# A hybrid SSM and attention block on one core: the GLU from two steps earlier, squares in tiles of their own, and some adds on another engine

## The chip, the core and the metric

The kernel runs on one core of a Trainium2 chip. The metric is device time in microseconds (us) for one execution. Three runs of the kernel before gave 1503.86, 1506.82 and 1508.20 us; the median is 1506.82. A fourth execution was profiled.

The engines are named as the profile names them: PE is TensorE's matmul and PEld its weight load, DVE is VectorE, ACT is ScalarE, POOL is GpSimd, SP is SyncE, which here only issues transfers. Each engine takes its instructions in the order in which the program holds them; an instruction that waits holds up those behind it on its engine. PSUM is the memory that matmuls write, held here as banks of 128 x 512 fp32; SBUF is the memory of tiles.

## What is computed

One layer over a sequence of 2048 tokens with 1024 channels, cut to what matters:

```python
hn = rmsnorm(h, mix_norm_g)
u, g_ssm, q, k, v, g_attn = split(hn @ w_in)              # six times 512 columns
y = s5_scan(u)                                            # diagonal complex state space model, 32 groups
val, gate = split(gelu(y + d * u) @ w_glu + b_glu)        # 512 -> 2 x 512
y_ssm = val * sigmoid(gate) * silu(g_ssm)
y_att = stick_breaking(rmsnorm(q), rmsnorm(k), v) * silu(g_attn)   # 8 heads of 64, causal
h = h + concat(y_ssm, y_att) @ w_out
h = h + sigmoid(rmsnorm(h, ple_norm_g) @ w_ple_gate) * (p @ w_ple_proj)
```

Stick-breaking attention needs, for each block of 128 queries, the scores, a running sum over the keys from the right (a scan on DVE) and a product with v.

## The kernel before

All matmuls of fp32 data are made of three: each operand is split into a high part (ACT, L513, or L491 where weights are scaled too) and a low part (DVE, L65 or L76) in a matmul format, and high x high, low x high and high x low are summed in PSUM (L541 to L543, and L707 to L709 for the last stages).

**Stages, in the time of the profiled execution.**
- 0 to about 148 us: `phase_u`. The row blocks T (256 tokens each) are loaded, and u = x @ w_in is computed by L541 to L543. The first row block is multiplied before its norm is known: `norms(i)` for its two halves (L573 to L586) computes the squares on ACT (L575), sums them by three adds on POOL (L577) and a matmul with ones (`ps_row`, L579), and spreads the row scale by a second matmul (L585) and an ACT copy (L586). The result scales u afterwards (DVE, `uq`). Later row blocks are normed first (`load_x`, L588 to L603): an ACT square with a sum (L596), a power on POOL (L507), an ACT scaling (L598), transposes on PE (`ps_x`, L526), and the split. Beside all this a long chain of small DVE operations prepares the constants of the scan (`ssm_chain`).
- to about 313 us: the state space model in batches and its output z, and the gate.
- about 313 to 1110 us: the attention loop, steps t = 0 to 39. Four pairs of heads follow each other, each 8 steps after the last, with 16 query blocks each; so two pairs overlap until t = 31, and only the last is left from t = 32. A block's scores go to PSUM (`ps_z`, L812), ACT takes the exponentials (L816), the DVE scans (`px`, L821), PE turns the weights (`ps_wt`, L526), ACT copies them (`ws`, L835), and PE multiplies them with v (`ps_o`, L843). The projections of later blocks (`ps_q`, L745) are laid between.
- In the last eight of these steps (`glu_at = steps - 8`) stands the GLU: 16 units, two each step. Every fourth one starts with `glu_z`, four loads of z (`zt`, two buffers) and their split to `zr` (ACT 513, DVE L65). A unit (`glu_unit`, L684 to L699) has 12 matmuls for the gate half (`ps_g`, bank "ssm") and 12 for the value half (`ps_v`, bank "acc"), a sigmoid on ACT (L696), a DVE multiply-add (L76), a product with the SSM gate on POOL (L698) and a store (L699). The GLU's weights (`wst<-in_ssm_w_glu_dram`) are loaded from step 29 on.
- In the same steps `cross_sums` (L861) makes, in eight groups, sums of blocks of w_out and w_ple_gate by four POOL subtractions each: the last two matrix products are done by a scheme with seven block products instead of eight, which needs such sums of the weights and of the activations.
- about 1110 to 1285 us: the product with w_out for pairs of query blocks (`mixed_pair`, matmuls `ps_h`). Its sums of activations, `sx`, are four POOL adds a pair (L912), split by ACT and DVE to `yr`; then `h<-h,u` on POOL (L969).
- to 1504 us: the gated layer (`gated_pair`, `ps_g`). Its last operations are a DVE product with the projection of p and a POOL add of h (L1026), then the store.

**What sets the order.** The code does not run in the order in which it is written. A planner (`plan`, `list_schedule`, `best_order`, `arrange`) lays out the instructions of each engine from a model of durations and the dependences between instructions, tile reuse among them. So each edit lets it lay out the neighbourhood anew. Tiles come from pools with a fixed count of buffers by tag; a tile that takes a buffer waits until everything that used the one before in it is done. The pool "w" is a ring of 16 weight tiles. The pool kv2 holds, for keys and values, the slots 2, 5, 6 and 7 of the attention; slots 2, 5 and 7 are last read by the third pair of heads, whose last block is at t = 31; slot 6 by the second pair, at t = 23. `BANKS` says which PSUM banks the scores, the projections and the outputs use; the GLU's steps use a set that leaves "ssm" to it.

Of the kernel before, what the change touches and what calls it, by code (L numbers as in the profile page):

```python
# [18 lines left out]
P = 128  # L19
# [7 lines left out]
L = 16  # L27
# [518 lines left out]
def phase_u(e, pool, xp, chain):  # L546
# [23 lines left out]
    ones = pool.tile([P, P], F32, tag="ones", name="ones")  # L570
    nc.gpsimd.memset(ones, 1.0)

    def norms(i):  # L573
        x, r = plain[i], e.rs[i]
        nc.scalar.activation(x, x, AF.Square)  # L575
        for n in (4, 2, 1):
            nc.gpsimd.tensor_tensor(x[:, :n], x[:, :n], x[:, n:2 * n], op=ALU.add)  # L577
        ps = e.bank("ps_row", "tr", "ssm")
        nc.tensor.matmul(ps[:, :1], x[:, 0], ones[:, :1], start=True, stop=True)  # L579
        vs(nc, r, ps[:, :1], 1.0 / DM, ALU.mult, EPS, ALU.add)  # L580
        nc.gpsimd.tensor_tensor(r, r, e.mhalf[:, :1], op=ALU.pow)
        d = pool.tile([P, P], F32, tag="dg", name="dg", bufs=1)
        vs(nc, d, e.ident, r, ALU.mult)
        ps = e.bank("ps_row", "tr", "ssm")
        nc.tensor.matmul(ps[:, :P], ones, d, start=True, stop=True)  # L585
        nc.scalar.activation(e.row[i // 2][:, i % 2 * P:i % 2 * P + P], ps[:, :P], AF.Copy)  # L586
# [84 lines left out]
def glu_z(e, pool, tb):  # L671

    zf = e.z_d.rearrange("j (k p) c -> p k j c", p=P)
    zr = pool.tile([P, 2, 4, 512], F32R, tag="zr", name="zr", bufs=1)
    for k in range(4):
        n = NCH // 4
        zt = pool.tile([P, L, n], F32, tag="zt", name="zt", bufs=2)
        e.nc.sync.dma_start(zt, zf[:, k, :, tb * n:(tb + 1) * n])
        hi, lo = (zr[:, s, k].rearrange("p (c j) -> p c j", j=L) for s in range(2))
        split(e, hi, lo, zt.rearrange("p j c -> p c j"))  # L680
    return zr


def glu_unit(e, pool, w, zr, tb, m):  # L684
    nc = e.nc
    gt = pool.tile([P, 512], F32, tag="gsm", name="gsm", bufs=2)
    nc.sync.dma_start(gt, e.gs_d[tb][m * P:(m + 1) * P])
    pg = e.bank("ps_g2", "ssm")
    pv = e.bank("ps_v2", "acc")
    cs = slice(m * P, (m + 1) * P)  # L690
    for half, ps in ((1, pg), (0, pv)):
        for c in range(4):
            wt = w[half][c]
            mm3(e, ps, (wt[:, 0, cs], wt[:, 1, cs]), (zr[:, 0, c], zr[:, 1, c]), c == 0, c == 3)
    sg = pool.tile([P, 512], F32, tag="glus", name="glus", bufs=2)
    nc.scalar.activation(sg, pg, AF.Sigmoid, bias=e.bglu[:, 4 + m:5 + m])  # L696
    stt(nc, sg, pv, e.bglu[:, m:m + 1], sg, ALU.add, ALU.mult)
    nc.gpsimd.tensor_tensor(sg, sg, gt, op=ALU.mult)  # L698
    nc.sync.dma_start(e.ys_d[tb][m * P:(m + 1) * P], sg)  # L699
# [158 lines left out]
    A.w += load_w(e, [cols[c, :, :, P * A.hp:P * (A.hp + 1)] for c in range(lo, hi)], 512, e.gmix, at=lo, **kw)  # L858


def cross_sums(e, pool, src, dst, scale, c):  # L861

    nc = e.nc
    t = []
    for i, j in ((0, 0), (0, 1), (1, 1), (1, 0)):
        a = pool.tile([P, 512], F32, tag="cs", name="cs", bufs=4)
        k = 4 * i + c
        nc.sync.dma_start(a, src[k * P:(k + 1) * P, 512 * j:512 * j + 512])
        if scale is not None:
            nc.scalar.activation(a, a, AF.Copy, scale=scale[:, k:k + 1])  # L870
        t.append(a)
    b11, b12, b22, b21 = t
    gp = nc.gpsimd.tensor_tensor
    gp(b11, b12, b11, op=ALU.subtract)
    gp(b12, b22, b12, op=ALU.subtract)
    gp(b22, b22, b11, op=ALU.subtract)
    gp(b21, b21, b22, op=ALU.subtract)
    for k, a in enumerate((b11, b22, b12, b21)):
        nc.sync.dma_start(dst[k][c * P:(c + 1) * P], a)
# [20 lines left out]
    return load_w(e, [d[c * P:(c + 1) * P] for c in range(4)], 512, None, **kw)  # L900


def cross_products(e, pool, name, q, w, early, late):

    nc = e.nc

    def f(tag, n):
        return pool.tile([P, 512], F32, tag=tag, name=tag, bufs=n)

    def add(a, b, op=ALU.add):  # L910
        t = f("sx", 3)
        nc.gpsimd.tensor_tensor(t, a, b, op=op)  # L912
        return t

    def product(ps, a, k, first):
        y = pool.tile([P, 2, 4, P], F32R, tag="yr", name="yr", bufs=4)
        split(e, y[:, 0].rearrange("p c t -> p (c t)"), y[:, 1].rearrange("p c t -> p (c t)"), a)
        for c in range(4):
            mm3x(e, ps, (y[:, 0, c], y[:, 1, c]), (w[k][c][:, 0], w[k][c][:, 1]), first and c == 0, c == 3, not first)

    ps = [e.bank(name, "z0", "z1", "acc", "ssm", "w0", "w1") for _ in range(4)]
    product(ps[0], q[0], 0, True)
    s1 = add(q[2], q[3])
    s2 = add(s1, q[0], ALU.subtract)
    r = f("r", 1)
    nc.scalar.activation(r, ps[0], AF.Copy)
    product(ps[1], s2, 1, True)
    u = f("u", 2)
    vt(nc, u, ps[1], r, ALU.add)
    product(ps[2], s1, 2, True)  # L930
    early(u, ps[2], 0)
    s3 = add(q[0], q[2], ALU.subtract)
    product(ps[3], s3, 3, True)
    early(u, ps[3], 1)
    product(ps[0], q[1], 4, False)
    late(0, ps[0], None)
    late(3, None, None)
    s4 = add(q[1], s2, ALU.subtract)
    product(ps[2], s4, 5, False)
    late(1, ps[2], u)  # L940
    product(ps[3], q[3], 6, False)
    late(2, ps[3], u)


def mixed_pair(e, pool, far, j):
# [31 lines left out]
        nc.scalar.activation(jk, h[k], AF.Square, accum_out=ss[:, i, m:m + 1])  # L977
        nc.sync.dma_start(e.h_d[2 * j + i][:, 512 * m:512 * m + 512], h[k])

    cross_products(e, pool, "ps_h", q, e.wo, early, late)  # L980
    r = pool.tile([P, 2], F32, tag=f"rs{j}", name="rs")
    vt(nc, r, ss[:, :, 0], ss[:, :, 1], ALU.add)
    vs(nc, r, r, 1.0 / DM, ALU.mult, EPS, ALU.add)
# [4 lines left out]
def gated_pair(e, pool, far, j, rs):  # L988
# [25 lines left out]
    def late(k, ps, u):  # L1014
# [8 lines left out]
        for c in range(2):  # L1023
            mm3x(e, pp, (pr[:, 0, c, ts], pr[:, 1, c, ts]), (e.wp[m][c][:, 0], e.wp[m][c][:, 1]), c == 0, c == 1)
        vt(nc, o[k], pp, o[k], ALU.mult)
        nc.gpsimd.tensor_tensor(o[k], o[k], h[k], op=ALU.add)  # L1026
        nc.sync.dma_start(e.out[0, (2 * j + i) * P:(2 * j + i + 1) * P, 512 * m:512 * m + 512], o[k])

    cross_products(e, pool, "ps_g", q, e.wg, early, late)
# [15 lines left out]
def hybrid_block_kernel(ctx: ExitStack, tc: tile.TileContext, x, xt, small, p, w_in, ssm_w_glu, w_out, w_ple_gate,  # L1045
# [121 lines left out]
    pk = pool(right, "pack", side="right")  # L1167
    early.close()
    e.stage = e.stage[:1]
    mid = ExitStack()  # L1170
    bp = pool(mid, "pb")
    with e.later():
        wgate = load_w(e, row_blocks(e.w_in[0], NC8, 512), 512, e.gmix)
# [39 lines left out]
    kv1 = pool(far, "kv1", side="right")  # L1213
    ap = pool(far, "attn", side="right")
    steps = NT + SKEW * (NHP - 1)
    glu_at = steps - 8
    for t in range(steps):
        e.z_banks, e.q_banks, e.o_banks = BANKS[2 if t < SKEW - 2 else t >= glu_at]
        for hp in range(NHP):
            if 0 <= t - SKEW * hp < NT:  # L1220
                attn_block(e, ap, A[hp], t - SKEW * hp)
        if t == glu_at:
            left.close()
            gl = pool(left, "glu")
            sums = pool(left, "sums")
        for hp in range(NHP):
            i = t - SKEW * hp
            if 0 <= i + 2 < NT and i + 2 >= (AHEAD if hp == 0 else 0):
# [5 lines left out]
        if t == AHEAD - 1:  # L1234
            left.close()
            e.xp = pool(ctx, "xp")
            kv2 = pool(left, "kv2")
            wx = pool(left, "wx")
        if t == glu_at - 3:
            wglu = glu_load(e)  # L1240
        if t >= glu_at:
            u = 2 * (t - glu_at)
            if u % 4 == 0:
                zr = glu_z(e, gl, u // 4)
            for k in range(u, u + 2):
                glu_unit(e, gl, wglu, zr, k // 4, k % 4)
            c = t - glu_at
            cross_sums(e, sums, *((w_out[0], e.so_d, None) if c < 4 else (w_ple_gate[0], e.sg_d, e.gple)), c % 4)
        if t == steps - 3:
            e.wo = [cross_weights(e, e.w_out[0], e.so_d, None, p) for p in range(2)]  # L1250
            wo4 = cross_weights(e, e.w_out[0], e.so_d, None, 4, pool=Halves(e))
    left.close()
    fin = pool(left, "fin")
    e.stage.append(pool(left, "fstage", 2))
# [354 lines left out]
```

## Time and profile before

| | us |
|---|---|
| median of three runs | 1506.82 |
| the profiled execution, time | 1506.30 |
| the profiled execution, span of the core | 1504.50 |
| PE busy | 1452.0 |
| DVE busy | 1010.2 |
| ACT busy | 811.4 |
| POOL busy | 486.2 |
| end of PE's last matmul | 1499.06 |

The mean granted TensorE clock of the profiled execution is 0.991. The span lies 1.8 us below the execution's time; what is said of places in the program is in microseconds from the span's start. A line such as `893.97 0.93 PE L812 MATMUL ps_z<-k,q ... x5 [1.50 <-DVE px L821]` is read: at 893.97 a group of five matmuls from line 812 starts, 0.93 us long, and before it the engine stood 1.50 us, until DVE's instruction on tile px from line 821 was done. In the table by stretch a row gives, for a stretch, each engine's busy time with the number of its instructions in brackets, then the granted clock, the share of the DMA engines' time and GB/s. A row of a tile's instructions gives count, shortest, median and longest in ns, and the start of the first and the last in us.

### The profile page before, as it was taken

How to read it: one execution, taken by the hardware profiler on the slowest of the kernel's cores; microseconds unless marked ns; L12 is line 12 of the kernel's file. 1: busy time of each engine (PE TensorE's matmuls, PEld its weight loads, DVE VectorE, ACT ScalarE, POOL GpSimd, SP SyncE). 2: the span in 40 equal slices, each digit the busy share in tenths (PEclk: the TensorE clock that was granted, in tenths of full speed). 3: DMA queues.
4: the chain of work that ended last, by engine and by line, in shares of the span. 5: the costliest groups of instructions: out<-in, count | busy, mean ns of one | idle time of the engine just before them, and what ended most of it. 6: DMA issues, size and time to landing. Idle time of an engine off the chain costs nothing.

```text
span 1504.5 us, 33553 instructions
## 1 busy us (share of the span) xinstructions
PE 1452.0 (97%) x13068; PEld 1223.9 (81%) x13068; DVE 1010.2 (67%) x1802; ACT 811.4 (54%) x1764; POOL 486.2 (32%) x524
## 2 busy tenths in 40 slices
PE   5999999999999999999999999999999999999998
PEld 5999989988888888887788877777777888777776
DVE  8943887976667876676766775547777557744544
ACT  5654545565556765566555665545654436533332
POOL 3221454422222112211112343432145555434433
PEclk9999999999999999999999989999999999999999
DMA  8877736644333423334233577653467446523221
GB/s 292 292 261 241 227 123 201 191 165 158 124 127 125 155 94 129 123 117 132 96 125 100 176 240 205 214 159 91 139 205 253 159 155 201 156 67 111 75 68 58
DMA packets 178909, 238.21 MB, mean 158 GB/s; under 512 B 65744, under 2 KB 121024, under 8 KB 167616
## 3 DMA queue, kind: packets, MB, share of 16 engines
q1 hardware_dynamic: 176368, 227.49, 47.1%
q0 software_dynamic: 2384, 8.59, 2.0%
q8 instruction: 103, 1.69, 0.5%
q14 instruction: 54, 0.44, 0.1%
HBM read 166.94 MB, written 64.90 MB: 154 GB/s over the span
## 4 chain that ended last, share of the span: by engine, by line
PE 75%; DVE 10%; issue 5%; DMA 4%; ACT 3%; POOL 1%; SPq 1%; POOLq 0%; DVEq 0%; ACTq 0%
PE ps_q L745 20%; PE ps_o L843 7%; PE ps_z L812 6%; PE ps_wt L526 4%; PE ps_h L709 3%; PE ps_h L707 3%; PE ps_h L708 3%; PE ps_g L707 3%; PE ps_g L709 3%; PE ps_g L708 3%; DMA wst<-in_ssm_w_glu_dram 1%; PE ps_u L541 1%; PE ps_u L543 1%; PE ps_u L542 1%; DVE px L821 1%
## 5 line engine op out<-in xcount | busy, mean ns | idle before, releaser
L821 DVE TENSOR_TENSOR_SCAN px<-px,ps_z 128x512 f32<-128x512 f32 (+3 forms) x320 | 338.9, 1085 | 105.4 <-ACT px L816 60.5
L745 PE MATMUL ps_q<-w_w,xt 64*128 64x512 f32 x2784 | 375.0, 399 | 2.4 <-DVE glus L76 1.6
L745 PEld LDWEIGHTS ps_q<-w_w,xt 64*128 64x128 f32 x2784 | 269.6, 186 | 43.0 <-DVE glus L76 1.7
L816 ACT ACTIVATE px<-ps_z 128x512 f32<-128x512 f32 (+3 forms) x320 | 159.2, 534 | 77.7 <-PE ps_z L812 76.1
L835 ACT ACTIVATE ws<-ps_wt 128x512 f32<-128x512 f32 (+3 forms) x320 | 160.2, 537 | 73.0 <-PE ps_wt L526 72.0
L812 PE MATMUL ps_z<-k,q 64*128 64x512 f32 (+3 forms) x960 | 143.2, 387 | 7.3 <-DVE px L821 6.2
L843 PE MATMUL ps_o<-ws,v 128*64 128x128 f32 x2176 | 137.7, 279 | 0.3 <-ACT ws L835 0.2
L843 PEld LDWEIGHTS ps_o<-ws,v 128*64 128x64 f32 x2176 | 119.4, 139 | 18.4 <-issue 14.1
L507 POOL TENSOR_TENSOR rs_qk<-rs_qk,mhalf 128x4 f32<-128x4 f32 x64 | 67.2, 1049 | 193.3 <-DVE rs_qk L72 193.1
L526 PEld LDWEIGHTS ps_wt<-ident,px 64*128 64x128 f32 x2176 | 96.9, 139 | 27.0 <-ACT ws L835 8.0
L812 PEld LDWEIGHTS ps_z<-k,q 64*128 64x128 f32 x960 | 88.8, 189 | 28.5 <-issue 8.7
L526 PE MATMUL ps_wt<-ident,px 64*128 64x64 f32 x2176 | 103.4, 225 | 4.4 <-ACT ws L835 3.8
L819 POOL TENSOR_SCALAR_AFFINE_SELECT px<-px 128x128 f32<-128x128 f32 x128 | 40.0, 324 | 166.4 <-ACT px L816 158.7
L756 POOL TENSOR_TENSOR v<-qn,v 128x128 f32<-128x128 f32 x64 | 31.0, 484 | 170.3 <-DMA v<-qn 148.0
L541 PE MATMUL ps_u<-xt,w_w 128*128 128x256 f32 x256 | 74.5, 293 | 8.2 <-ACT w_w L491 6.9
L1026 POOL TENSOR_TENSOR sg<-sg,h 128x512 f32<-128x512 f32 x32 | 44.3, 1395 | 114.6 <-DVE sg L65 105.4
L543 PE MATMUL ps_u<-xt,w_w 128*128 128x256 f32 x256 | 73.4, 293 | 2.7 <-DVE w_w L76 2.7
L542 PE MATMUL ps_u<-xt,w_w 128*128 128x256 f32 x256 | 74.0, 290 | 0.5 <-DVE xt L65 0.5
L65 DVE TENSOR_TENSOR yr<-sx,yr 128x512 fp32r<-128x512 f32 x64 | 48.4, 780 | 34.8 <-ACT yr L513 33.8
L513 ACT ACTIVATE yr<-sx 128x512 fp32r<-128x512 f32 x64 | 39.2, 629 | 54.6 <-POOL sx L912 21.3
L65 DVE TENSOR_TENSOR qn<-ps_q,part 128x512 f32<-128x512 f32 x54 | 36.8, 682 | 42.2 <-ACT part L751 39.3
L65 DVE TENSOR_TENSOR yr<-yq,yr 128x512 fp32r<-128x512 f32 x48 | 53.5, 1115 | 12.4 <-ACT yr L513 12.4
(434 smaller groups left out, 3467.7 us busy)
## 6 DMA issues: line engine op xcount, KB each, us to landing
xt<-hn SPq DMA_DIRECT2D x58, 1024.0 KB
hn<-xt SPq DMA_DIRECT2D x16, 1024.0 KB
h<-h SPq DMA_DIRECT2D x64, 256.0 KB
wst<-in_w_in_dram SPq DMA_DIRECT2D x48, 256.0 KB
xg<-hn SPq DMA_DIRECT2D x12, 1024.0 KB
out_dram<-sg SPq DMA_DIRECT2D x32, 256.0 KB
x<-in_x_dram SPq DMA_DIRECT2D x14, 512.0 KB
h<-in_x_dram SPq DMA_DIRECT2D x28, 256.0 KB
```

Of the source, the lines that this page charges most:

```text
L65: nc.vector.tensor_tensor(out, a, b, op=op)
L526: e.nc.tensor.transpose(ps[h][:, 64 * k:64 * k + 64], v[r], e.ident[r, r])
L541: mm(out, wh, xh, start=first, stop=False)
L707: mm(out, xh, wh, start=first, stop=False, skip_group_check=more)
L708: mm(out, xh, wl, start=False, stop=False, skip_group_check=more)
L709: mm(out, xl, wh, start=False, stop=last, skip_group_check=more)
L745: nc.tensor.matmul(o, xt[r, a, c], A.w[c][r, b], start=c + s == 0, stop=c == NC8 - 1 and s == 2)
L812: nc.tensor.matmul(z[:, :n], q[half[h], a], A.k[ch][half[h], b, :n], start=s == 0, stop=s == 2)
L816: nc.scalar.activation(px[:, :n], z[:, :n], AF.Sigmoid, scale=-(HD ** -0.5))
L821: nc.vector.tensor_tensor_scan(rv, rv, z[:, :n][:, ::-1], initial=1.0 if carry[h] is None else carry[h], op0=ALU.mult, op1=ALU.bypass)
L835: nc.scalar.activation(dst, ps, AF.Copy, bias=1.0, scale=-1.0)
L843: nc.tensor.matmul(po[half[h], :P], A.v[sb][:, h], w[:, h, b], start=sb == i, stop=sb == 0)
```

## The change

Four edits, each of which lets the planner lay out anew:

1. `norms()` writes its squares and their sums to two tiles of their own from the ring "w", no longer over x.
2. The GLU starts at step 30 (`steps - 10`), its units spread over ten steps (two, two, one, one, one, one, two, two, two, two). Its gate rows and sigmoids and the rows of `cross_sums` have no buffers of their own any more; they lie in key slots of kv2 whose keys are done: slot 6 alone in steps 30 and 31, slots 6 and 7 from 32 on, slots 2 and 5 for `cross_sums`, which starts at step 32 as before. `zt` has three buffers, not two. The GLU's pool takes the place of the pool wx at step 30. The bank set of the GLU's steps holds from step 30, too.
3. In the first two `mixed_pair`s the four `sx` adds are on DVE, not POOL.
4. In the last `gated_pair` the four last adds are on DVE, not POOL.

```diff
+    squares = [e.wpool.tile([P, NC8, P], F32, tag="w", name="sq") for hf in range(2)]
+
     def norms(i):
-        x, r = plain[i], e.rs[i]
-        nc.scalar.activation(x, x, AF.Square)
+        x, r = squares[i], e.rs[i]
+        nc.scalar.activation(x, plain[i], AF.Square)
...
-        zt = pool.tile([P, L, n], F32, tag="zt", name="zt", bufs=2)
+        zt = pool.tile([P, L, n], F32, tag="zt", name="zt", bufs=3)
...
-def glu_unit(e, pool, w, zr, tb, m):
+def glu_unit(e, old, slots, w, zr, tb, m):
     nc = e.nc
-    gt = pool.tile([P, 512], F32, tag="gsm", name="gsm", bufs=2)
+    both = old(slots[m % len(slots)])
+    gt, sg = both[:, 0], both[:, 1]
...
-    sg = pool.tile([P, 512], F32, tag="glus", name="glus", bufs=2)
...
-def cross_sums(e, pool, src, dst, scale, c):
+def cross_sums(e, old, src, dst, scale, c):
...
-    for i, j in ((0, 0), (0, 1), (1, 1), (1, 0)):
-        a = pool.tile([P, 512], F32, tag="cs", name="cs", bufs=4)
+    rows = [b[:, k] for b in (old(2), old(5)) for k in range(2)]
+    for (i, j), a in zip(((0, 0), (0, 1), (1, 1), (1, 0)), rows):
...
-def cross_products(e, pool, name, q, w, early, late):
+def cross_products(e, pool, name, q, w, early, late, eng=None):
...
-        nc.gpsimd.tensor_tensor(t, a, b, op=op)
+        (eng or nc.gpsimd).tensor_tensor(t, a, b, op=op)
...
-    cross_products(e, pool, "ps_h", q, e.wo, early, late)
+    cross_products(e, pool, "ps_h", q, e.wo, early, late, nc.vector if j < 2 else None)
...
-        nc.gpsimd.tensor_tensor(o[k], o[k], h[k], op=ALU.add)
+        (nc.vector if j == NT // 2 - 1 else nc.gpsimd).tensor_tensor(o[k], o[k], h[k], op=ALU.add)
...
-    mid = ExitStack()
+    mid, over = ExitStack(), ExitStack()
...
-    glu_at = steps - 8
+    glu_units = [[0,1],[2,3],[4],[5],[6],[7],[8,9],[10,11],[12,13],[14,15]]
+
+    def old(slot):
+        return kv2.tile([P, 2, 512], F32, tag=f"k{slot}", name="old", bufs=1)
+
+    glu_at = steps - 10
...
-            left.close()
-            gl = pool(left, "glu")
-            sums = pool(left, "sums")
+            over.close()
+            gl = pool(over, "glu")
...
-            wx = pool(left, "wx")
-        if t == glu_at - 3:
+            wx = pool(over, "wx")
+        if t == glu_at - 1:
             wglu = glu_load(e)
         if t >= glu_at:
-            u = 2 * (t - glu_at)
-            if u % 4 == 0:
-                zr = glu_z(e, gl, u // 4)
-            for k in range(u, u + 2):
-                glu_unit(e, gl, wglu, zr, k // 4, k % 4)
-            c = t - glu_at
-            cross_sums(e, sums, *((w_out[0], e.so_d, None) if c < 4 else (w_ple_gate[0], e.sg_d, e.gple)), c % 4)
+            for k in glu_units[t - glu_at]:
+                if k % 4 == 0:
+                    zr = glu_z(e, gl, k // 4)
+                glu_unit(e, old, (6, 7) if t >= glu_at + 2 else (6,), wglu, zr, k // 4, k % 4)
+            c = t - glu_at - 2
+            if c >= 0:
+                cross_sums(e, old, *((w_out[0], e.so_d, None) if c < 4 else (w_ple_gate[0], e.sg_d, e.gple)), c % 4)
...
+    over.close()
```

The diff shifts later lines by two: line 743 before is line 745 now.

**How it moves instructions.** PE's order is new from the start to about 370 us, the same from there to about 840, new again to 1110, and nearly the same after. ACT at the start, before (`xt<-x` is the high split of the first row block, `w_w` a weight, L575 the square of its one half, L596 that of a later block):

```order
L513 ACTIVATE xt<-x 128x256 x2
L575 ACTIVATE x<-x 128x1024
L491 ACTIVATE w_w<-wst,gmix 128x512 x2
L575 ACTIVATE x<-x 128x1024
L596 ACTIVATE jk,ss<-x 128x1024 x2
L598 ACTIVATE x<-x,rs_x 128x1024
```

and now, the square being L577:

```order
L513 ACTIVATE xt<-x 128x256 x2
L491 ACTIVATE w_w<-wst,gmix 128x512 x2
L577 ACTIVATE sq<-x 128x1024 x2
L598 ACTIVATE jk,ss<-x 128x1024 x2
L600 ACTIVATE x<-x,rs_x 128x1024
```

The last two weights' splits come ahead of both squares. PE a little ahead of the first GLU unit, before, with only scores, turned weights and outputs (about 897 to 907 us in the trace):

```order
L812 MATMUL ps_z<-k,q 128x512 x6
L526 MATMUL ps_wt<-ident,px 128x64 x16
L812 MATMUL ps_z<-k,q 128x512 x6
L843 MATMUL ps_o<-ws,v 64x128 x16
L526 MATMUL ps_wt<-ident,px 128x64 x16
L812 MATMUL ps_z<-k,q 128x512 x6
```

and now, a piece two score groups ahead of these:

```order
L543 MATMUL ps_v_14430<-zr,w_w 128x512
L541 MATMUL ps_g_14818<-zr,w_w 128x512
L526 MATMUL ps_wt<-ident,px 128x64 x12
L845 MATMUL ps_o<-ws,v 64x128 x16
L542 MATMUL ps_g_14818<-zr,w_w 128x512
L814 MATMUL ps_z<-k,q 128x512 x6
L526 MATMUL ps_wt<-ident,px 128x64 x16
L747 MATMUL ps_q<-w_w,xt 128x512 x18
```

Matmuls of two GLU units (`ps_v`, `ps_g`) stand among the attention's. On SP the loads for them stand, now, like this (`zt` is z, `wst` with w_glu a GLU weight, `xt<-hn`, `v<-qn` and `ya` belong to the attention):

```order
L849 DMA ya_110<-yat 128x128
L680 DMA zt<-z 128x16x32 x3
L486 DMA wst<-in_ssm_w_glu_dram 128x1x512
L719 DMA xt<-hn_68 128x2048
L755 DMA v<-qn 127x128
L486 DMA wst<-in_ssm_w_glu_dram 128x1x512
```

Three loads of z precede the last two GLU weights; before, all weights were issued ahead of any z.

## The prediction

> **What bounds the kernel now.** I read the page's busy shares and chain first, then the stretches, then the rows inside those stretches where TensorE (PE) is not full.
>
> ```profile
> span 1504.5 us, 33553 instructions
> PE 1452.0 (97%) x13068; PEld 1223.9 (81%) x13068; DVE 1010.2 (67%) x1802; ACT 811.4 (54%) x1764; POOL 486.2 (32%) x524
> PE 75%; DVE 10%; issue 5%; DMA 4%; ACT 3%; POOL 1%; SPq 1%; POOLq 0%; DVEq 0%; ACTq 0%
> ```
>
> PE works 1452.0 of 1504.5 us, and three quarters of the chain that ended last is PE itself. The change removes no matmul, so it can only win from the 52.5 us in which PE stands, or from time in which PE runs slowly. The table by stretch says where those are (columns: busy time and, in brackets, instructions of each engine, then the granted TensorE clock, the DMA share and GB/s):
>
> ```profile
> 25.00:35.00 10.00, 5.00 (x50) 3.74 (x48) 10.00 (x45) 5.96 (x12) 3.71 (x7) 0.82 0.81 270
> 35.00:75.00 40.00, 39.26 (x368) 37.85 (x369) 39.85 (x169) 25.87 (x46) 9.31 (x11) 0.96 0.86 299
> 150.00:370.00 220.00, 214.64 (x1883) 197.53 (x1884) 179.05 (x318) 124.37 (x292) 85.90 (x68) 1.00 0.58 178
> 370.00:840.00 470.00, 463.00 (x5772) 391.98 (x5770) 326.42 (x576) 280.89 (x692) 91.20 (x174) 1.00 0.37 122
> 840.00:885.00 45.00, 43.97 (x570) 36.12 (x568) 35.90 (x56) 30.64 (x73) 17.73 (x23) 1.00 0.67 219
> 885.00:930.00 45.00, 39.41 (x446) 30.95 (x443) 29.37 (x37) 28.36 (x57) 18.79 (x21) 0.85 0.74 212
> 930.00:1111.00 181.00, 177.02 (x1536) 140.19 (x1534) 111.91 (x149) 100.70 (x198) 54.95 (x58) 1.00 0.54 156
> 1111.00:1165.00 54.00, 49.94 (x233) 38.93 (x234) 41.70 (x50) 25.04 (x51) 32.68 (x25) 1.00 0.78 253
> 1165.00:1480.00 315.00, 311.56 (x1382) 246.66 (x1381) 173.52 (x234) 134.82 (x246) 141.47 (x104) 1.00 0.39 123
> ```
>
> Three stretches that the change touches are poorly filled: 25 to 35 (5.0 us idle), 885 to 930 (45 − 39.41 = 5.6 idle, and a granted clock of only 0.85) and 1111 to 1165 (4.1 idle). The second is the largest, because the lower clock is a second loss: 0.15 x 45 = 6.75 us of clock withheld, so up to 5.6 + 6.75 = 12.3 us lie there, somewhat less where the two overlap. From 370 to 840 the order of PE's instructions is the same in both programs, so I put that stretch at nothing.
>
> **The GLU, two steps sooner.** What stops PE there:
>
> ```profile
> 893.97 0.93 PE L812 MATMUL ps_z<-k,q 64*128 64x512 f32 x5 [1.50 <-DVE px L821]
> 900.23 1.64 PE L812 MATMUL ps_z<-k,q 64*128 64x512 f32 x5 [0.62 <-DVE px L821]
> 913.17 0.55 PE L812 MATMUL ps_z<-k,q 64*128 64x128 f32 x5 [1.39 <-DVE px L821]
> 921.97 0.50 PE L541 MATMUL ps_g<-zr,w_w 128*128 128x512 f32 x1
> 922.54 0.39 PE L543 MATMUL ps_g<-zr,w_w 128*128 128x512 f32 x1
> 922.77 0.40 PE L541 MATMUL ps_g<-zr,w_w 128*128 128x512 f32 x1
> ...
> 890.00:900.00 10.00, 7.60 (x81) 5.80 (x77) 7.70 (x12) 5.89 (x15) 4.97 (x6) 0.75 0.74 230
> 900.00:910.00 10.00, 9.12 (x106) 7.35 (x107) 5.79 (x7) 4.70 (x10) 6.05 (x7) 0.74 0.52 179
> ```
>
> Scores wait for the DVE scan that has to free their bank, and PE, which takes its work in order, has nothing else to do: the first GLU matmul comes only at 921.97. The 2.4 us idle between 890 and 900 are followed by a lowered clock: 0.74 between 900 and 910 although PE is 9.12 of 10 busy there. A GLU matmul follows the last by 922.77 − 922.54 = 0.23 us, so a unit of 24 is 5.5 us, and the four units that now stand in steps 30 and 31 bring 22 us of work that needs no scan. In the changed order three to twelve of them stand between nearly all the score groups that before stood there alone. That is four times what the 5.6 us of gaps need, and with the gaps the lowered clock should go as well. It will not be all: a piece of GLU ahead of a score group also delays that group's scan, and the pieces aren't sized to each gap. I take two thirds of the ceiling, 8 us.
>
> [...]
>
> Against this stand two costs. The sixteen units are now spread over ten steps, one each in four steps of the middle: 1111 − 930 loses filler. PE was idle only 3.98 of 181 us there; with 33 us of the 89 us of GLU gone ahead (six units), about a third less, I put 0.7 on it, up to 2. And the loads for the GLU come sooner:
>
> ```profile
> 855.27 0.63 ACT L513 ACTIVATE w_w<-wst 128x512 fp32r<-128x512 f32 x1 [2.12 <-DMA wst<-in_ssm_w_glu_dram]
> 870.57 0.63 ACT L513 ACTIVATE w_w<-wst 128x512 fp32r<-128x512 f32 x1 [0.73 <-DMA wst<-in_ssm_w_glu_dram]
> L513 ACT ACTIVATE zr<-zt x16: 1088/1129/1179, 915.3 to 1068.9; 128x512 fp32r<-128x512 f32 x16
> ```
>
> ScalarE (ACT) already stood 2.12 and 0.73 us for the last two GLU weights. On SyncE's queue three loads of z are now issued ahead of those two, and four splits of 1.13 us on ACT move into a stretch where PE had only 1.0 of 45 us idle. Nothing shows such a stall coming to the scores; I put 1.5 us on it, between 0 and 2.85 of standing plus 4.5 of splits, 7.4. The term is −8 + 0.7 + 1.5 = −5.8, bounds −12.3 and +9.4 (nothing filled, 2 and 7.4 lost).
>
> **The squares.** Before, ACT squares the first two row blocks over x itself, so it waits for the DVE to finish its low split of x; now it does not.
>
> ```profile
> 19.58 1.06 ACT L575 ACTIVATE x<-x 128x1024 f32<-128x1024 f32 x1 [3.79 <-DVE xt L65]
> 20.72 4.68 POOL L577 TENSOR_TENSOR x<-x 128x512 f32<-128x512 f32 x4 [14.37 <-ACT x L575]
> 27.20 1.15 ACT L598 ACTIVATE x<-x,rs_x 128x1024 f32<-128x1024 f32 x1 [2.17 <-POOL rs_x L507]
> 33.77 0.58 PE L541 MATMUL ps_u<-xt,w_w 128*128 128x256 f32 x1 [1.17 <-ACT xt L513]
> 33.54 1.28 DVE L65 TENSOR_TENSOR xt<-ps_x,xt 128x512 fp32r<-128x512 f32 x2
> 34.87 0.58 PE L542 MATMUL ps_u<-xt,w_w 128*128 128x256 f32 x1 [0.52 <-DVE xt L65]
> ```
>
> ACT stood 3.79 us. GpSimd's (POOL's) sums, the row scale that they hold up, and the next block's turn could all move up by at most that, less where the weights' split (kept ahead of the squares in the new order) fills it: up to 3 us at 34.87. But the DVE is full, 10.00 of 10 and then 39.85 of 40 us, with the same long chain of small operations ahead of the splits, and PE is 39.26 of 40 busy right after. A matmul that may start sooner then waits for the DVE's split later. I take 0, bounds −3 and +3. The shift also makes the planner lay out 35 to 370 anew; of the 5.4 us idle from 150 to 370 it can win or lose some 3, and I take 0.
>
> **The adds that go to the DVE.**
>
> ```profile
> 1113.99 1.28 POOL L912 TENSOR_TENSOR sx<-yq 128x512 f32<-128x512 f32 x1 [7.76 <-DMA yq<-ya]
> 1115.35 1.59 POOL L912 TENSOR_TENSOR sx<-sx,yq 128x512 f32<-128x512 f32 x1
> 1117.66 0.50 PE L707 MATMUL ps_h<-w_w,yr 128*128 128x512 f32 x1 [1.94 <-ACT yr L513]
> 1119.86 2.31 DVE L65 TENSOR_TENSOR yr<-yq,yr 128x512 fp32r<-128x512 f32 x1
> 1130.24 0.68 DVE L65 TENSOR_TENSOR w_wc<-wst,w_wc 128x512 fp32r<-128x512 f32 x1
> ...
> 1498.88 2.48 POOL L1026 TENSOR_TENSOR sg<-sg,h 128x512 f32<-128x512 f32 x2 [4.75 <-DVE sg L65]
> 1498.12 0.68 DVE L65 TENSOR_TENSOR sg<-ps_p,sg 128x512 f32<-128x512 f32 x1
> ```
>
> PE stands 1.94 us for two POOL adds of 1.28 and 1.59 and ACT's split behind them. The DVE does this size in 0.68: 2 x 0.68 instead of 2.87 saves 1.5 us. The eight adds put 8 x 0.68 = 5.4 us on a DVE that is 41.70 of 54 busy; 47.1 of 54 still fits. The bounds: −2.5, if later gaps of the stretch go too, to +2, if the DVE's 2.31 us case (beside a POOL add, against 0.68) befalls one or two of the adds on the path. I take −1.5. [...]
>
> At the end the last add, half of 2.48, becomes 0.68: −0.6, bounds −0.8 and 0.
>
> **The sum.** 1506.3 (the profiled execution, 0.5 below the median of the runs, 1506.82) − 5.8 + 0 − 1.5 − 0.6 = 1498.4; against the median 1498.9. I say 1498.5.
>
> **The rivals.** *A: the gain is hidden.* What PE gains at 885 to 930 it waits for later, since the attention of the last head pair goes on as a chain of scan after scan and the steps with one unit hold less to lay between. For it: the page gives DVE 10% of the chain. Against it: PE is 177.02 of 181 us full afterwards, and a full engine keeps what it gained. Only the adds and a rest of 1 us are left: 1506.3 − 2.1 − 1 = 1503.
>
> *B: everything fits.* All of the 12.3, no loss by loads, and 2 us at the start: 1506.3 − 12.3 − 2 − 2.1 = 1490. Against it: the gaps are many, and each must meet its piece.
>
> *C: the first units stall in order.* In steps 30 and 31 only K's slot 6 holds gate and sigmoid, so unit k+1's sigmoid on ACT waits until unit k's product has been stored.
>
> ```profile
> L696 ACT ACTIVATE glus<-ps_g,bglu x16: 678/689/720, 932.5 to 1097.7; 128x512 f32<-128x512 f32 x16
> L76 DVE SCALAR_TENSOR_TENSOR glus<-ps_v,bglu,glus x16: 722/746/754, 936.0 to 1100.7; 128x512 f32<-128x512 f32 x16
> L698 POOL TENSOR_TENSOR glus<-glus,gsm x16: 1272/1288/2036, 936.8 to 1101.6; 128x512 f32<-128x512 f32 x16
> ```
>
> From a unit's last matmul it takes 0.75 + 1.29 and the store, for which the end of the kernel gives 3.1 us (the last add ends at 1498.88 + 2.48 = 1501.36, the span at 1504.5): 5.1 us. The next unit's gate half is 12 x 0.23 = 2.8 us. Where units stand back to back ACT waits 2.3 us, and behind the sigmoid in its queue stand the exponentials and evictions that the scores and the weights' turns need, so PE waits as well. Three handovers are 6.9 us, and if the clock then halves for two stretches like the one at 900 (0.26 x 10 us each), 5.2 more. With nothing gained there but the adds: 1506.3 + 6.9 + 5.2 − 2.1 = 1516. It decides from about 1 us a handover, with filling half as good as I take it. Against it: attention pieces stand between the units, which give the store its time.
>
> *D: the start.* The new layout of the first 370 us loses its 3 + 3 us and the GLU only half fills (−1): 1506.3 + 6 − 1 − 2.1 = 1509.
>
> **How the numbers follow.** Forecast 0.45 (own range 1494 to 1502), A 0.16, B 0.10, C 0.22, D 0.07. About 4.5 us (0.3%) is what a measurement of this kernel tells from no change: below 1502.3 is faster, above 1511.3 slower. Forecast and B are faster, 0.55. A ends within it, and so do half of D's scatter around 1509 and the mildest of C, 0.05 together: same is 0.21, slower the rest, 0.24. The range 1489 to 1512 holds all but C's heavier half and the best of B.
>
> **What would show it.** Right: the stretch of the old 885 to 930 (score groups 720 to 810) with under 2 us of idle and a granted clock near 1.00, GLU matmuls between scores, 930 to the end of attention no emptier than before; the first L707 of the output phase waiting under 0.5 us; the last add 0.7 us on the DVE. Wrong: ACT waiting for a store ahead of a sigmoid, or for the GLU weights by more than 3 us; the clock below 1.00 between 840 and 885; DVE adds of some 2 us between yq's landing and L707; the 35 us mark later than before by over 1 us and not regained by 370.

## The result and the profile after

The changed kernel ran 1514.25 us (median of five runs, 1510.76 to 1518.53), the kernel before beside it 1504.87 (1503.86 to 1508.2): a ratio of 1.0058, 95% interval 1.0035 to 1.0081. It is slower, by about 9 us. The forecast was 1498.5, faster than before, in a range from 1489 to 1512.

The profiled execution took 1513.79 us. Its page, the lines that answer to those shown of before:

```profile
span 1512.0 us, 33579 instructions
PE 1456.3 (96%) x13068; PEld 1229.6 (81%) x13068; DVE 1018.4 (67%) x1814; ACT 813.4 (54%) x1764; POOL 465.9 (31%) x512
PE 73%; DVE 11%; DMA 5%; issue 4%; ACT 3%; POOL 3%; SPq 0%; POOLq 0%; DVEq 0%; ACTq 0%
```

PE's idle time is 55.7 us, 3 more than before, and PE's busy time is 4.3 us longer for the same 13068 matmuls, at a mean granted clock of 0.988 against 0.991. The table by stretch (busy time and count of PE, PEld, DVE, ACT, POOL, then granted clock, DMA share, GB/s) says where:

```profile
0.00:25.00 25.00, 15.20 (x78) 13.92 (x79) 20.79 (x107) 13.94 (x24) 11.13 (x22) 0.93 0.72 254
25.00:35.00 10.00, 5.81 (x59) 4.95 (x59) 9.06 (x49) 4.76 (x8) 2.23 (x4) 0.77 0.94 331
35.00:75.00 40.00, 36.77 (x336) 34.93 (x337) 38.39 (x167) 25.89 (x46) 7.74 (x10) 0.93 0.79 277
75.00:150.00 75.00, 75.00 (x677) 73.14 (x674) 31.80 (x49) 33.76 (x66) 14.36 (x13) 0.98 0.76 245
150.00:370.00 220.00, 204.31 (x1671) 188.66 (x1669) 174.54 (x301) 118.64 (x276) 79.18 (x60) 0.98 0.55 173
370.00:840.00 470.00, 464.60 (x5782) 394.03 (x5782) 325.36 (x577) 280.94 (x691) 93.11 (x177) 1.00 0.37 124
840.00:885.00 45.00, 40.50 (x503) 33.76 (x500) 32.18 (x50) 29.25 (x67) 6.47 (x13) 0.99 0.51 123
885.00:930.00 45.00, 45.00 (x457) 35.50 (x457) 29.62 (x42) 23.20 (x52) 7.37 (x12) 0.94 0.42 118
930.00:1111.00 181.00, 178.78 (x1652) 140.91 (x1654) 121.30 (x157) 107.61 (x216) 77.74 (x78) 1.00 0.65 194
1111.00:1165.00 54.00, 51.37 (x378) 41.38 (x375) 43.38 (x62) 32.28 (x64) 20.16 (x19) 1.00 0.84 271
```

Two of these rows of before, which were not shown yet:

```profile
0.00:25.00 25.00, 14.64 (x90) 12.99 (x91) 20.10 (x113) 13.99 (x24) 9.55 (x20) 1.00 0.81 291
75.00:150.00 75.00, 74.46 (x683) 71.91 (x682) 33.05 (x53) 36.61 (x74) 14.25 (x13) 1.00 0.74 250
```

From 150 to 370 us PE is busy 204.31 of 220, where it was 214.64: 10.3 us more idle, with 0.98 of the clock where it had all of it. (The later rows lie some 19 us later in the program than the same rows of before.) How late the program is can be read at one instruction that both have, in the part with the same order; PE's timeline of before:

```profile
396.08 0.72 PE L526 MATMUL ps_wt<-ident,px 64*128 64x64 f32 x16 [0.67 <-ACT ws L835]
```

and of the changed kernel:

```profile
415.62 0.72 PE L526 MATMUL ps_wt<-ident,px 64*128 64x64 f32 x16 [0.67 <-ACT ws L837]
```

19.5 us late, after the same idle 0.67. At the end the span is only 7.5 longer (1512.0 − 1504.5): 12 us are made up after this place. So two things were to be explained: a loss of 20 in the first 370 us, and a gain of 12 behind it. Over the five rows up to 370 us PE idles 10.9 us more than before (−0.6, −0.8, +2.5, −0.5 and +10.3), and the lowered clock withholds some 9 us more (1.8, 0.5, 1.2, 1.5 and 4.4, each the difference of the clocks times the stretch). Together that is 20 for the 19.5, a little too much, since some of the slow time was idle too. The clock terms of the single short rows are weak evidence: in the traces of before and e2, which have the same order there, the clock from 25 to 35 us is 0.82 and 0.67.

### The profile page after: what moved, and what is told of

Read it like the earlier page. It is cut to its first block, busy times and chain, and to the rows that moved or that the text cites. A ratio compares the mean times of both kernels' runs of the same rounds, so it can differ in the third digit from the quotient of the medians.

```text
span 1512.0 us, 33579 instructions
## 1 busy us (share of the span) xinstructions
PE 1456.3 (96%) x13068; PEld 1229.6 (81%) x13068; DVE 1018.4 (67%) x1814; ACT 813.4 (54%) x1764; POOL 465.9 (31%) x512
## 4 chain that ended last, share of the span: by engine, by line
PE 73%; DVE 11%; DMA 5%; issue 4%; ACT 3%; POOL 3%; SPq 0%; POOLq 0%; DVEq 0%; ACTq 0%
PE ps_q L747 20%; PE ps_o L845 7%; PE ps_z L814 6%; PE ps_wt L526 4%; PE ps_g L709 4%; PE ps_g L711 4%; PE ps_g L710 3%; PE ps_h L711 3%; PE ps_h L709 3%; PE ps_h L710 3%; DMA wst<-in_ssm_w_glu_dram 2%; PE ps_u L542 1%; PE ps_u L543 1%; PE ps_u L541 1%; DMA v<-qn 1%
## 5 line engine op out<-in xcount | busy, mean ns | idle before, releaser
L814 PE MATMUL ps_z<-k,q 64*128 64x512 f32 (+3 forms) x960 | 138.9, 383 | 6.4 <-DVE px L823 3.2
L541 PE MATMUL ps_u<-xt,w_w 128*128 128x256 f32 x256 | 76.5, 300 | 7.4 <-ACT w_w L491 6.2
L543 PE MATMUL ps_u<-xt,w_w 128*128 128x256 f32 x256 | 74.8, 298 | 3.6 <-DVE w_w L76 3.6
L542 PE MATMUL ps_u<-xt,w_w 128*128 128x256 f32 x256 | 76.7, 301 | 0.6 <-DVE xt L65 0.6
L1028 POOL TENSOR_TENSOR sg<-sg,h 128x512 f32<-128x512 f32 x28 | 39.3, 1412 | 99.7 <-DVE sg L65 90.7
L541 PEld LDWEIGHTS ps_u<-xt,w_w 128*128 128x128 f32 x256 | 52.7, 206 | 7.9 <-ACT w_w L491 6.2
```

What stands on the lines that cost most here:

```text
L541: mm(out, wh, xh, start=first, stop=False)
L542: mm(out, wh, xl, start=False, stop=False)
L814: nc.tensor.matmul(z[:, :n], q[half[h], a], A.k[ch][half[h], b, :n], start=s == 0, stop=s == 2)
```

## The experiments

**e1 and e2: which edit loses, which gains.** e1 is the kernel before with

```diff
+    squares = [e.wpool.tile([P, NC8, P], F32, tag="w", name="sq") for hf in range(2)]
-        x, r = plain[i], e.rs[i]
-        nc.scalar.activation(x, x, AF.Square)
+        x, r = squares[i], e.rs[i]
+        nc.scalar.activation(x, plain[i], AF.Square)
```

and e2 the changed kernel with just this undone.

> The kernel before with the first edit alone (squares in two tiles of the weights' ring). The changed kernel's trace is 19.5 us late at 415 us, at the same PE instruction. Theory S (the loss belongs to the squares' edit): the whole loss is here, 1504.9 + 18 = about 1523 (1518 to 1527), and nothing is gained back later. Rival G (part of the loss comes from the GLU's edit, by its tiles or loads): under 1512.

> The changed kernel with the first edit undone (squares over x again). Theory S: the start is as before, and what the other three edits gain stays: from 415 us on the changed kernel made up 19.5 - 8.2 = 11 us, so about 1494 (1491 to 1498). Rival: the 11 us were slack that any late start gives back, then about 1503 to 1506.

Measured: e1 1525.47 us, ratio 1.0140 (1.0122 to 1.0158); e2 1494.08 us, ratio 0.9928 (0.9910 to 0.9945). The squares' edit alone costs 21 us, the other three gain 11, and the product of the two ratios, 1.0067, is that of the whole change within its interval. e2 is faster than both kernels.

**e3 and e4: the tiles or the order.** The squares' edit changes neither the number of instructions nor their numbering, so the order that the planner gives to one program can be put on the other, as a kept list:

```diff
-    _, order, _ = best_order(ops, pre, *rest, rows)
+    order = kept_order()
```

e3 is the kernel before, with squares over x, and the order of e1. e4 has the order of before, and squares in tiles of their own; so that the weights' ring "w" keeps its turns, they take two turns of the ring `uq`:

```diff
-        x, r = plain[i], e.rs[i]
-        nc.scalar.activation(x, x, AF.Square)
+        r = e.rs[i]
+        x = pool.tile([P, L, NCH // 2], F32, tag="uq", name="sq", bufs=4).rearrange("p j c -> p (j c)").rearrange("p (k t) -> p k t", k=NC8)
+        nc.scalar.activation(x, plain[i], AF.Square)
```

> The kernel before, its squares over x as before, but every engine's instructions in the order that the planner gives for the squares' edit alone. Theory O (the new order of the first 370 us costs, not the tiles): as e1, within 4 us, about 1523. Rival T (the squares' place in the ring costs, by later weights that wait for their slots): within 5 us of before, about 1505.

> The kernel before with the squares in two tiles of the ring uq (not of the weights' ring, which keeps its turn), and every engine's instructions in the order of the kernel before. Theory O: no loss; ACT no longer waits 3.79 us for x, so the start may be up to 3 us earlier: 1502 to 1506. Rival (a square outside x costs by itself, by port or memory): 1508 or more.

Measured: e3 1524.33 us, ratio 1.0129 (1.0108 to 1.0150); e4 1505.67, ratio 1.0004 (0.9989 to 1.0018). The order alone, on the old tiles, costs the whole loss within the intervals; own tiles under the old order cost and gain nothing that can be told. e4 does not show what a square without any wait would gain, since ACT waits there for the ring's earlier user (ACT's timeline of e4):

```profile
21.16 1.06 ACT L576 ACTIVATE sq<-x 128x1024 f32<-128x1024 f32 x1 [3.76 <-DVE w_w L76]
```

The changed kernel has that case, with no wait ahead of the squares, and shows where the freed time went (ACT's timeline):

```profile
17.24 1.99 ACT L577 ACTIVATE sq<-x 128x1024 f32<-128x1024 f32 x2
...
27.14 1.15 ACT L600 ACTIVATE x<-x,rs_x 128x1024 f32<-128x1024 f32 x1 [5.69 <-POOL rs_x L507]
```

The next step, the scaling of x, started at 27.20 before and starts at 27.14 now: ACT waits 5.69 us for the row scale instead of 2.17. The matmul that the prediction showed at 34.87 comes 1.5 us later (PE's timeline):

```profile
36.38 0.58 PE L542 MATMUL ps_u<-xt,w_w 128*128 128x256 f32 x1 [0.60 <-DVE xt L65]
```

That is one of the prediction's own signs of being wrong: the 35 us mark more than 1 us late, and not regained by 370.

**e5 and e11: the GLU and the adds apart.** e5 is the kernel before with the second edit alone, e11 with the third and fourth alone (their diffs stand in the change).

> The kernel before with the second edit alone (GLU two steps sooner, key slots, three zt). Of the 11.5 us that the three edits of e2 gained, the prediction gave 1.5 to the sx adds and 0.6 to the last adds. If that holds, the GLU alone gives 9.4: about 1496 (1493 to 1498). Rival (the adds carry more, as 1111 to 1165 lost 3.7 us of idle in e2): 1499 to 1501.

> The kernel before with the third and fourth edit alone (sx adds of the first two mixed pairs and the last four adds on the DVE). e2 against e5 makes them 4.6 us, if the edits add up: 1500 (1498.5 to 1501.5). Rival (they are worth the prediction's 1.5 + 0.6, and the rest of the 4.6 belongs to their meeting with the GLU's new place): 1502 to 1503.

Measured: e5 1498.67 us, ratio 0.9963 (0.9948 to 0.9978), 5.6 us; e11 1500.78 us, ratio 0.9956 (0.9940 to 0.9972), 6.6 us with an interval of 4.2 to 9.0. e5 falls between what the two theories had; e11 decides for the rival, the adds carry more than the prediction gave them. The table by stretch of e11, and two rows of its DVE:

```profile
1111.00:1165.00 54.00, 54.00 (x256) 43.41 (x255) 40.15 (x60) 26.25 (x54) 23.88 (x17) 1.00 0.79 248
```

```profile
1108.57 0.69 DVE L912 TENSOR_TENSOR sx<-yq 128x512 f32<-128x512 f32 x1 [0.95 <-DMA yq<-ya]
1109.30 0.69 DVE L912 TENSOR_TENSOR sx<-sx,yq 128x512 f32<-128x512 f32 x1
...
1121.69 1.78 DVE L912 TENSOR_TENSOR sx<-yq 128x512 f32<-128x512 f32 x1
```

PE is full there, 54.00 of 54 against 49.94 before: 4.1 us, all the idle time of the stretch and not only the 1.5 ahead of one product. The first adds took 0.69 us each; one later add, beside POOL's `h<-h,u`, took 1.78, without harm to PE.

**e8: the late GLU weight.** In e2 PE's one long stand from 840 to 885 us is where the GLU begins (e2's timeline: the last weight's issue on SP, then rows of ACT and PE):

```profile
850.76 4.53 SPq L486 DMA_DIRECT2D wst<-in_ssm_w_glu_dram  x1
861.45 0.63 ACT L513 ACTIVATE w_w<-wst 128x512 fp32r<-128x512 f32 x1 [3.84 <-DMA wst<-in_ssm_w_glu_dram]
861.99 0.58 ACT L751 ACTIVATE part<-ps_q 128x512 f32<-128x512 f32 x1
863.34 0.50 PE L541 MATMUL ps_g<-zr,w_w 128*128 128x512 f32 x1 [2.77 <-DVE qn L65]
```

The releaser named for PE is DVE's `qn`, which is made from `part`; and `part` stood on ACT right behind the last weight, for which ACT had waited 3.84 us. e8 is e2's kernel, but the planner may issue the first loads of z only behind that weight:

```diff
             wglu = glu_load(e)
+            rows.append((len(nc.cur_bb.bb.instructions) - 3, 9, "mark"))
...
-        e.nc.sync.dma_start(zt, zf[:, k, :, tb * n:(tb + 1) * n])
+        with e.later(9):
+            e.nc.sync.dma_start(zt, zf[:, k, :, tb * n:(tb + 1) * n])
```

> Kernel of e2 (no squares' edit), and the first loads of z are issued only behind the last GLU weight, which in e2 lands late (ACT waits 3.84 us for it, PE 2.77 us idle, then half the clock for 3.4 us). Theory L (the loads of z ahead of it delay the weight): ACT's wait for it is under 1 us, and 2 to 4.5 us are saved: 1490 to 1492. Rival: z itself comes late and the first units wait for zr instead: 1494 or more.

Measured: 1493.64 us, ratio 0.9927 (0.9903 to 0.9951), the same as e2. SP, ACT and PE in e8's timeline:

```profile
852.24 2.75 SPq L486 DMA_DIRECT2D wst<-in_ssm_w_glu_dram  x1
853.57 0.63 ACT L513 ACTIVATE w_w<-wst 128x512 fp32r<-128x512 f32 x1 [2.57 <-DMA wst<-in_ssm_w_glu_dram]
861.15 0.64 ACT L513 ACTIVATE w_w<-wst 128x512 fp32r<-128x512 f32 x1 [0.37 <-DMA wst<-in_ssm_w_glu_dram]
875.38 1.07 ACT L513 ACTIVATE zr<-zt 128x512 fp32r<-128x512 f32 x1 [3.81 <-DMA zt<-z]
876.66 0.48 PE L526 MATMUL ps_tq<-ident,qn 64*128 64x64 f32 x4 [3.02 <-ACT g L792]
878.56 0.80 PE L541 MATMUL ps_g<-zr,w_w 128*128 128x512 f32 x1
```

The last weight's wait fell to 0.37 us, but the weight itself came no sooner: ACT takes it at 861.15, and took it at 861.45 in e2. Its issue ends at 854.99 here and at 855.29 in e2, so it needed 6.2 us from there in both, with the loads of z ahead of it or not. That z delayed the weight, theory L, is not what happened. What came late instead was z, as the rival had it: ACT stood 3.81 us for it at 875.38, the copy `g` that PE waits for is behind that on ACT, and PE stood 3.02 us. The first GLU matmul came at 878.56, 15 us later than in e2. The stall moved; it was not removed.

**e6, e7, e10, e15: where the order loses.** All four are the kernel before with its squares over x; the order of each engine is that of one program up to what PE has begun at some time, and that of the other behind it.

> The kernel before (squares over x); every engine in the order of the squares' edit up to what PE has begun at 75 us, and from there in the order of the kernel before. Theory H2 (most of the 20 us is lost by the layout after 75 us, where gate matmuls come ahead of the last of U and the packing): late by the 4 to 6 us that e3 is late at 75, about 1510 (1507 to 1513). Rival H1 (the first 75 us set the delay that grows later by itself): 1517 or more.

> The kernel before; the order of the kernel before up to 75 us, and from there that of the squares' edit. Theory H2: keeps the loss after 75 us, about 1519 (1515 to 1522). Rival H1: 1505 to 1508.

> As e7, but the order of the kernel before up to the first output matmul of the state space model (158 us there), and from there that of the squares' edit. Theory F: within 4 us of before, 1503 to 1509. Rival W: 1512 or more.

> As e10, but the order of the kernel before up to what PE has begun at 260 us, and from there that of the squares' edit. In e10 PE idled 9 us more than before between 200 and 330 us, 7 of it after 270. If that late part is bad by its own order: 1511 to 1520. If it is bad only because of what went ahead (150 to 260 us): 1504 to 1508.

| | order | ratio (95%) |
|---|---|---|
| e3 | new throughout | 1.0129 (1.0108 to 1.0150) |
| e6 | new to 75 us, then old | 1.0024 (1.0003 to 1.0044) |
| e7 | old to 75 us, then new | 1.0083 (1.0054 to 1.0112) |
| e10 | old to 158 us (the model's first output matmul), then new | 1.0106 (1.0084 to 1.0128) |
| e15 | old to 260 us, then new | 1.0066 (1.0045 to 1.0086) |

The first 75 us cost 3.6 us by e6, and 6.9 by what e3 has more than e7; H2 holds. The rest is in what comes after 158 us, since e10 loses no less than e7; and e15 puts 10 us of it into the last stretch, 260 to 370, by its own order: nothing ahead of it was changed. What a seam between two orders costs by itself was not tested; e6, which has one at 75 us, loses 3.6 us with it. What PE waits for between 150 and 370 us (the view of waits: in all, times, longest), before:

```profile
PE ps_q L745 <- DVE gsq L65: 1.6, 1, 1.6
...
PE ps_y L461 <- ACT tp L455: 0.6, 1, 0.6
...
PE ps_y L461 <- DVE gsq L65: 0.3, 1, 0.3
```

in the changed kernel:

```profile
PE ps_y L461 <- ACT tp L455: 3.7, 3, 2.3
PE ps_z L814 <- DVE sg L65: 2.0, 1, 2.0
PE ps_y L461 <- DVE gsq L65: 1.8, 2, 0.9
PE ps_z L814 <- DVE px L823: 1.3, 2, 0.9
PE ps_pack L340 <- DVE bn L65: 1.2, 1, 1.2
```

and in e15:

```profile
PE ps_y L461 <- ACT tp L455: 2.9, 2, 2.3
PE ps_z L812 <- DVE sg L65: 2.0, 1, 2.0
PE ps_y L461 <- DVE gsq L65: 1.8, 2, 0.9
PE ps_z L812 <- DVE px L821: 1.3, 2, 0.9
```

These are mostly waits of the state space model's last outputs (`ps_y`) and of the first scores behind them, each a microsecond or two in which PE, in its order, had nothing else. The clock is lower there as well. From 150 to 370 us it is 1.00 in the traces of before, e2, e4, e5 and e11, which have the old order there, and 0.98 in those of the changed kernel and of e15. The clock records of before hold no time at half the clock in this stretch; those of the changed kernel hold 10.2 us, which withholds up to 5.1 us.

**e9 and e16: two guesses at what in the order does it.** In e7's order 41 gate matmuls stand ahead of the last 36 of U and the first packing; e9 puts them behind. In e10's order gate matmuls were left over behind the waits; e16 brings the last two units of the gate, and what they need, some 6 us forward. Both are kept lists, the diff is that of e3.

> e7 with one thing moved: the first 41 gate matmuls, which in e7 stand ahead of the last 36 matmuls of U and the first four packing matmuls, come behind them (with three evictions and a store that depend on them); all else in e7's order. Theory F (these gate matmuls delay the state space model's start, and all of its chain): more than half of e7's 12.4 us comes back, 1505 to 1510. Rival W (the loss is spread over the order after 150 us): 1514 to 1518.

> e10's order with the last two units of the gate (and what they need) about 6 us earlier among the rest, so that gate matmuls stand in the places where PE idles from 265 to 330 us, and not behind them. Theory G (left-over gate matmuls are the missing filler): 4 to 9 us faster than e10, 1514 to 1520. Rival: no faster than 1522.

Measured: e9 1519.38 us, ratio 1.0079 (1.0062 to 1.0095) against e7's 1.0083: no change, theory F falls. e16 1544.03 us, ratio 1.0249 (1.0223 to 1.0275) against e10's 1.0106: much slower, theory G falls in this form. The view of waits of e16, 150 to 370 us, shows the longest waits:

```profile
PE ps_pack L347 <- ACT stB L341: 7.2, 1, 7.2
PE ps_y L464 <- DVE rot L65: 6.9, 2, 5.2
PE ps_sg L541 <- DVE sg L65: 6.3, 3, 2.4
```

The longest of them can be followed one step back, in ACT's and PE's timeline:

```profile
278.15 0.38 ACT L659 ACTIVATE sg<-ps_sg 128x256 f32<-128x256 f32 x1 [11.49 <-DMA gs<-sg]
279.07 1.08 PE L347 MATMUL ps_pack<-bn,cts 128*32 128x256 f32 x8 [7.15 <-ACT stB L341]
```

A gate eviction on ACT stood 11.49 us until a store of an earlier gate tile (`gs<-sg`) was done, and `stB`, for which PE stood, is right behind it on ACT. So e16 shows what this hand-made order ran into, a tile that was not free yet, and tells little about the gate as filler: from 150 to 370 us ACT waits 0.5 us in all for that store in the changed kernel, and this one wait in e16 is 11.49.

**e12, e13, e14: is it the squares, or any new layout?** e12 has e4's tiles, laid out by the planner itself. e13 and e14 change no operation and no tile, only one constant of the planner's model each, which lays out mainly the first 370 us anew:

```diff
-        return (0.05 if psum else 0.094) + n * 0.00083, 0.065 if psum else 0.03
+        return (0.05 if psum else 0.0941) + n * 0.00083, 0.065 if psum else 0.03
```

```diff
-def list_schedule(ops, pre, soft, length, mode, rank, near=4.0, change=0.09):
+def list_schedule(ops, pre, soft, length, mode, rank, near=4.0, change=0.091):
```

> The kernel before with the squares in two tiles of the ring uq, laid out by the planner itself (e4 had the old order). In its order the last of U and two groups of packing stand ahead of the first gate matmul, as before. Theory F: 1504 to 1510. Rival (any new layout of these 370 us loses, since the one before was the best of many): 1515 or more.

> The kernel before, all tiles and operations as they were; in the planner's table ACT's fixed part is 0.0941 us in place of 0.094. It then lays out the first 370 us anew. Theory R (the order before was a good one by luck, any new layout loses): slower by 5 to 20 us, 1510 to 1525. Rival Q (a new layout costs nothing by itself; the squares' edit led to a bad one): 1502 to 1508.

> As e13, with another constant: the planner's price for a change of PE's tile mode is 0.091 us in place of 0.09, which also lays the first 370 us out anew, in another way. Theory R: 1510 to 1525. Rival Q: 1502 to 1508.

Measured: e12 1515.37 us, ratio 1.0049 (1.0033 to 1.0066); e13 1516.95, ratio 1.0076 (1.0051 to 1.0101); e14 1507.46, ratio 1.0020 (1.0004 to 1.0036). The row 150 to 370 of e13's table by stretch:

```profile
150.00:370.00 220.00, 207.96 (x1741) 191.75 (x1741) 175.07 (x305) 119.47 (x278) 82.09 (x63) 0.98 0.52 165
```

A tenth of a nanosecond in the planner's table costs 11 us, most of it in the same 150 to 370 us (207.96 busy against 214.64, with 0.98 of the clock against 1.00). All four new layouts, those of e1, e12, e13 and e14, lose: 21, 7, 11 and 3 us. So theory R holds in the main, these new layouts lose by themselves, squares or not. e14 is the weakest witness: its 1507.46 us lie in the range that the rival, Q, had, and only the ratio's interval (0.6 to 5.4 us) puts it above no change. Whether the squares in the weights' ring lead to a worse layout than others would, four layouts do not tell.

## Why the prediction was wrong

- **The step that failed** is the one sentence on the new layout: "The shift also makes the planner lay out 35 to 370 anew; of the 5.4 us idle from 150 to 370 it can win or lose some 3, and I take 0." Its size was read from the idle time that the stretch had. That bounds a gain, not a loss: PE was 214.64 of 220 busy in an order that happened to fit, and a new order lost 10.3 us of idle time there and some clock (0.98 against 1.00). e1 and e3 make this term +21 and +19 us.
- **Rival D** had the place and the mechanism of the loss, at 6 us in place of 20, and a chance of 0.07; the GLU that only half fills, its other half, did not come.
- **The squares' wait** was taken at 0, with −3 to +3, because the DVE is full there. In the changed kernel the net stays inside these bounds: ACT's wait is gone, the scaling of x starts at the same time (27.14), where it waits for POOL's `rs_x` and not for the DVE, and the matmul of 34.87 comes 1.5 us later. e4's 1.0004 speaks for the tiles alone, since ACT still waits 3.76 us there.
- **The GLU** was taken at −5.8; e5 measured −5.6 (−3.3 to −7.8). That the two agree is partly luck, since its terms were off in both directions. Two rows of e5's table by stretch, which starts from the old order:

```profile
840.00:885.00 45.00, 40.56 (x429) 31.54 (x427) 32.42 (x53) 26.12 (x60) 8.39 (x12) 0.96 0.63 145
885.00:930.00 45.00, 45.00 (x505) 36.37 (x507) 26.05 (x31) 24.84 (x49) 13.49 (x17) 1.00 0.42 142
```

  The filling is complete, 45.00 of 45 at 1.00: all of the 12.3 us of the trace of before, where two thirds, 8, were taken. (Of these the clock's 6.75 us are at the high end: with the same order e4's trace has 0.89 there, for 0.85, and e11's has 0.98 from 840 to 930, for 0.92.) Against it the start of the GLU cost more than the 1.5 us put on the loads: from 840 to 885 PE idles 4.4 us instead of 1.0, and the clock is 0.96 instead of 1.00, some 5 us in all, inside the bound of 7.4. In e2 it is the late weight, with 3.84 us on ACT, 2.77 on PE and half the clock behind it; in the changed kernel ACT waits 4.3 us for that weight, above the 3 us that the prediction named as a sign of being wrong. The reason given, loads of z ahead of the weights, is not borne out by e8. The price for less filler later, 0.7, does not show in PE's share: e5 is 177.37 of 181 busy from 930 to 1111, against 177.02.
- **Rival C** fell. ACT's waits in the changed kernel, 870 to 960 us (in all, times, longest):

```profile
ACT w_w L513 <- DMA wst<-in_ssm_w_glu_dram: 5.5, 2, 4.3
...
ACT old L698 <- issue: 2.0, 2, 1.2
```

  The sigmoids (L698) were held 2.0 us in all, and PE was full from 885 to 930; the stop at the start of the GLU stood behind the weight.
- **The adds** were right in mechanism and under-sized: −1.5 and −0.6 against e11's −6.6 (−4.2 to −9.0). The term counted the one wait of 1.94 us; the edit filled all 4.1 us idle of the stretch. The case that its upper bound names, 2.31 us beside a POOL add, decided nothing: the first adds took 0.69 us, and beside the one of 1.78 PE stayed full. In the changed kernel the last add took 0.69 too, and the time from PE's last matmul to the span's end fell from 5.4 to 4.7. Some 2 us of e11's gain, within its interval, were not placed. Part of it may be the clock where the edit changes nothing (0.98 against 0.92 from 840 to 930 in the two traces).

What stays open: which instructions of the order between 150 and 370 us make the difference. The splices give the stretches, the view of waits the instructions that wait; the two hand-made orders that were to show the cause did not, and e16 tripped over a store. That the three edits without the squares are faster, and by how much, is shown (e2, 0.9928).

## What to carry to other kernels

Where a planner sets the order of every engine, price an edit twice: what it does by itself, and what a fresh layout of its neighbourhood may cost, which is not bounded by the idle time that the old layout had. Measure that second price with a null edit, such as a last digit in the planner's table, before an edit is judged; here it was 3 to 11 us, as large as what the edits were worth. And put an edit on the kept old order where the program allows it: that separates the tiles from the order in one run.

## What the hardware showed that was not expected

A lowered clock was seen right behind short waits. Two rows of e2's table by stretch, around the one wait of 2.77 us:

```profile
858.00:864.60 6.60, 3.57 (x51) 2.64 (x47) 2.38 (x4) 3.15 (x7) 0.70 (x2) 1.00 0.70 140
864.60:868.00 3.40, 3.40 (x34) 3.28 (x36) 2.21 (x5) 1.75 (x4) 1.01 (x1) 0.50 1.00 327
```

PE is full again in the second, 3.40 of 3.40, at half the clock.

The clock records of the traces of before and of the changed kernel say more. Every stretch at half the clock in them lasts 3.41 us or two or three times that, but for the one that the end of each trace cuts off. With the two traces cut into pieces of 3.41 us along these records, PE's idle time in each piece at full clock shows what comes before a lowered clock. Where PE stood 1.19 us or less, the next piece was never at half the clock; where it stood 2.10 us or more, the next one always was; between 1.24 and 1.74 both occur. The same holds in e2: in the 3.41 us ahead of its half clock, 861.2 to 864.6, PE stood 2.40 us. So in these traces it is the standing within one such piece that goes with the lowered clock, not the length of a single wait: in the changed kernel the wait of 2.30 us that ends at 308.23 lies in two pieces, with 1.04 and 1.27 us of standing, and the clock stayed full; in the trace of before the wait of 1.50 us that ends at 893.97 lies in one, and the half clock starts at 894.94. One piece at half the clock withholds up to 1.7 us. No run varied one wait alone to test this. It fits that executions with the same order of PE differ: from 885 to 930 the clock was 0.85 in the trace of before and 0.89 in e4's.

Idle time in these full stretches came with a loss of clock of nearly its size: up to 370 us the changed kernel idles 10.9 us more, and its records hold 27.3 us at half the clock, against 6.8 before, which withholds up to 10.2 us more.
